# Retention's value and gate projections as seven block products

## The chip, the cores and the metric

One Trainium2 chip, one of its cores. The time is device microseconds (us) of one execution of the kernel. The engines are PE (TensorE, matmuls; PEld its weight loads), DVE (VectorE), ACT (ScalarE), POOL (GpSimd) and SP (which here only issues DMAs). Each executes its own queue in order and waits on semaphores for the others.

## The reference

One decoder layer for 512 tokens of width 1024: four retention heads beside four attention heads of 128, each query attending to its best 128 keys as an indexer chooses them, then an output projection, layer norm, a SwiGLU FFN and a second norm. Cut to what matters here:

```python
proj = x @ w_in                       # 512 x 1024 times 1024 x 4168
rq, rk, rv, rg, aq, ak, av, iq, ik, iw = jnp.split(proj, IN_SPLITS, axis=-1)
ret = retention_chunkwise(rope(rq), rope(rk), rv)      # chunks of 128 tokens
ret = (ret - mean(ret)) * rsqrt(var(ret) + 1e-5) * ret_gn_gain   # per head
ret = silu(rg) * ret
sel = top_k(sum_h(iw * relu(iq_h . ik)), 128)          # causal, per query
att = softmax_attention(rope(aq), rope(ak), av, sel)
mix = concatenate([ret, att]) @ w_out
x = layer_norm(ALPHA * x + mix)
ffn = (silu(x @ w_gate) * (x @ w_up)) @ w_down
return layer_norm(ALPHA * x + ffn)
```

Here rv (values) and rg (gate) are each x times a 1024 x 512 part of `w_in`.

## The kernel before

Nearly all matmuls work on fp32 numbers split into two fp32r parts, high and low (`split`: ACT casts the high part; the low part is the rest). `mm3` makes one product of three matmuls: high by high, high by low, low by high. In `stream` each weight array has two letters, one for each half of 1024 columns: with V the low part is a DVE subtraction (L91); with Q it is made by ACT (minus the number) and a DMA from POOL's queue that adds the number to it (L88, L89).

Stages around the change, in PE's order:

- The indexer's projection (`acc`), then `proj_feature` for c = 0 to 7: keys and queries of both groups, two halves each, 24 matmuls a half into a `pf` bank. Behind each half DVE makes three rotary products (L217 to L219) and POOL adds them (L221).
- `proj_token(1)` (retention's values rv), `proj_token(2)` (its gate; `sg` and `grg`), `proj_token(0)` (attention's values av): each takes eight weight halves, and each half feeds 24 matmuls into four `pt` banks, one for each block of 128 tokens.
- Beside them runs `side`: rotation of the indexer, its logits (PE `lg`, ACT relu, DVE sum into `score`) for query blocks 1 to 3, then `topk`: 16 steps for each block of MAX8 and MATCH_REPLACE8 on DVE, over 256, 384 and 512 keys. `retention()` is a list of steps on all engines (transposed keys `rkt`, scores `rs`, state `rkv`, output `ri`, norm, scale, gate, turn).

All of it is one thread of code that issues instructions to every engine; each engine keeps the order of issue. `run(main, pace(side, r))` steps `main` and after each of its yields takes as many steps of `side` as its costs and the rate r allow. `weight()` hands out the next half and issues the preparation of the one three ahead (`prepare`); the raw arrays rotate through three buffers, the split halves through four. DMAs from HBM are issued on SP's queue in the order of issue.

Of the kernel before, what the change touches and what calls it, by code (L numbers as in the profile page):

```python
# [53 lines left out]
def hybrid_layer_kernel(ctx: ExitStack, tc: tile.TileContext, xT, x, pos, w0, wf, wt, wo,  # L54
# [30 lines left out]
    def split(eng_lo, hi, lo, src):  # L85
        A.copy(hi, src)  # L86
        if eng_lo is None:
            A.activation(lo, src, AF.Copy, scale=-1.0)  # L88
            nc.gpsimd.dma_start(lo.bitcast(F32), src, accum_op=ALU.add)  # L89
        else:  # L90
            eng_lo.tensor_tensor(lo, src, hi.bitcast(F32), op=ALU.subtract)  # L91
# [77 lines left out]
        yield  # L169


    stream = [(wf[c], "VV" if c == 0 else "VQ") for c in range(8)]
    stream += [(wt[g, i], "QQ") for g in (1, 2, 0) for i in range(2)]
    stream += [(wo[c], "VV") for _ in range(2) for c in range(4)]
    limit = [len(stream)]
    ready, taken, raws = [], [0], []

    def fetch(n):
        while len(raws) < min(n, limit[0]):
            raws.append(wp.tile([P, 2, 1024], F32, tag="raw", name=f"raw{len(raws)}"))  # L180
            dma(raws[-1], stream[len(raws) - 1][0])

# [50 lines left out]
    def index_rope():  # L233
# [105 lines left out]

    tok = {}  # L340

    def proj_token(g):
        accs = [(psu if g == 1 and b > 1 else psd)(f"pt{g}_{b}") for b in range(NB)]

        def evac(b):
            if b == 0:
                tok[g] = unit(("s4", "s5", "s6")[g], ("av", "rv", "grg")[g])
            if g == 2:
                sg = tmp("sg")
                A.activation(sg, accs[b], AF.Silu)  # L350
                G.tensor_tensor(tok[g][:, b], sg, gnb, op=ALU.mult)
            else:
                A.copy(tok[g][:, b], accs[b])

        for c in range(4):
            h, l = weight()
            for b in range(NB):
                bs = slice(b * P, b * P + P)
                for k in range(2):
                    kt = 2 * c + k  # L360
                    ks = slice(k * S, k * S + S)
                    mm3(accs[b], xh[kt][:, bs], xl[kt][:, bs], h[:, ks], l[:, ks], kt == 0, kt == KT - 1)
                settle()
                if c == 3:
                    pending.append(lambda b=b: evac(b))
# [113 lines left out]
    def ret_state(b):  # L479
        kv = psu(f"rkv{b}")  # L480
        for h in range(HEADS):
            hs = slice(h * P, h * P + P)
            T.matmul(kv[:, hs], lhsT=rt["k", b][:, hs], rhs=tok[1][:, b, hs], start=True, stop=True)
        new = rt["state", b + 1] = tmp(f"rstate{b}")
        if b == 0:
            A.copy(new, kv)
        else:
            G.tensor_tensor(heads(new), heads(rt["state", b]), per_head(8), op=ALU.mult)
            V.tensor_tensor(new, new, kv, op=ALU.add)

    def ret_out(b, pair):
        if pair == 0:
# [9 lines left out]
    def ret_norm(b):  # L502
        st = sp.tile([P, 4, 6], F32, tag="st", name="st")
        mv = sp.tile([P, 4, 2], F32, tag="mv", name="mv")
        for h in range(HEADS):
            V.bn_stats(st[:, h], rt[b][:, h * P:(h + 1) * P])
        for h in range(HEADS):
            V.bn_aggr(mv[:, h], st[:, h])
        rt["norm", b] = mv, rstd_of(mv[:, :, 1], 4)

    def ret_scale(b):
        mv, r = rt["norm", b]
        z = tmp("rz")
        for h in range(HEADS):
            hs = slice(h * P, h * P + P)
            V.tensor_scalar(z[:, hs], rt[b][:, hs], mv[:, h, 0:1], r[:, h:h + 1], op0=ALU.subtract, op1=ALU.mult)
        rt[b] = z

    def ret_gate(b):
        zz = tmp("rzz")  # L520
        G.tensor_tensor(zz, rt[b], tok[2][:, b], op=ALU.mult)
        rt[b] = zz

    def ret_turn(b):
# [65 lines left out]
    prepare()  # L590
    prepare()
    const_loads()
    lg = chain(*[logits(j) for j in range(1, NB)])
# [5 lines left out]
    rt["decay"] = big.tile([P, 2, HEADS * P], F32, tag="s7", name="decay")  # L599
    dma(rt["decay"], decay_d)  # L600
# [1075 lines left out]
```

## Time and profile before

| what | value |
|---|---|
| time, median of 3 runs | 614.81 us (614.14 to 614.89) |
| profiled execution | 614.91 us, span 613.1 us |
| granted PE clock | 0.996 of full speed |
| features: first to last `pf` start | about 27 to 123 us |
| token projections (`pt`) | 123.8 to 207 us |
| DVE top-k steps (L402, L403) | 48 of each |
| low parts by ACT and POOL's DMA (L88, L89) | 19 |
| low parts by DVE (L91, 128x1024 weights) | 24 |

How to read it: the page gives busy time and counts of each engine, the chain of work that ended last, and groups of equal instructions with count, busy time, mean ns of one, and the idle time before them with the engine that ended it. The timeline shows the start, the duration and the instruction.

### The profile page before, as it was taken

The page shows a single profiled execution, that of the slowest core. Times are in us where ns is not written, and L with a number is a line of the kernel's source. Part 1 is how long each engine was busy: PE and PEld are TensorE (multiplying, and loading weights), DVE is VectorE, ACT ScalarE, POOL GpSimd, SP SyncE. Part 2 cuts the span into 40 slices and gives each one's busy share as a digit, 9 for nine tenths or more (in the row PEclk, how much of TensorE's full clock was granted, in tenths as well). Part 3 has the DMA queues.
Part 4 walks back from the last instruction along what each step waited for, and adds up shares of the span by engine and source line. Part 5 has one row for each costly group of instructions (what it writes and reads, how often), then busy time and mean ns, then how long its engine had stood idle before and what let it go on. Part 6 is the DMA issues. An engine that isn't in the chain of part 4 may idle for free.

```text
span 613.1 us, 9090 instructions
## 1 busy us (share of the span) xinstructions
PE 603.2 (98%) x3228; PEld 518.2 (85%) x3228; DVE 523.3 (85%) x973; ACT 350.1 (57%) x610; POOL 160.0 (26%) x171
## 2 busy tenths in 40 slices
PE   8999999999999999999999999999999999999994
PEld 7988888888888877889998888888888888888884
DVE  6897687987879877979998999999999899977856
ACT  5643444334252665777657767677677795648300
POOL 1187232421446000232123223231321021124010
PEclk9999999999999999999999999999999999999998
DMA  8878434788553773498399998988786459689502
GB/s 296 299 219 206 152 107 124 179 193 207 134 123 103 276 275 136 106 238 156 121 264 199 246 210 216 217 208 240 175 225 171 138 175 246 165 230 300 190 35 103
DMA packets 41805, 116.53 MB, mean 190 GB/s; under 512 B 4464, under 2 KB 10160, under 8 KB 36128
## 3 DMA queue, kind: packets, MB, share of 16 engines
q1 hardware_dynamic: 23056, 80.95, 38.0%
q0 software_dynamic: 17968, 33.76, 31.7%
q10 hardware_dynamic: 736, 1.25, 0.6%
q8 instruction: 25, 0.41, 0.3%
q14 instruction: 20, 0.16, 0.1%
HBM read 83.96 MB, written 2.10 MB: 140 GB/s over the span
## 4 chain that ended last, share of the span: by engine, by line
PE 89%; DVE 5%; issue 3%; ACT 1%; POOL 1%; DMA 1%; POOLq 0%; DVEq 0%
PE ga L905 11%; PE ga L908 6%; PE gc L905 5%; PE pf L95 5%; PE pf L94 5%; PE pf L96 5%; PE acc L205 4%; PE gb L905 3%; PE gc L908 3%; PE ga L915 3%; PE mx L96 2%; PE mx L94 2%; PE mx L95 2%; PE dl L94 2%; PE dl L95 2%
## 5 line engine op out<-in xcount | busy, mean ns | idle before, releaser
L86 ACT CAST wh<-raw 128x1024 fp32r<-128x1024 f32 x43 | 44.9, 1049 | 49.1 <-issue 21.6
L94 PE MATMUL pf<-xh,wh 128*128 128x512 f32 x128 | 50.0, 391 | 0.0
L95 PE MATMUL pf<-xl,wh 128*128 128x512 f32 x128 | 49.9, 390 | 0.0
L96 PE MATMUL pf<-xh,wl 128*128 128x512 f32 x128 | 49.9, 389 | 0.0
L91 DVE TENSOR_TENSOR wl<-raw,wh 128x1024 fp32r<-128x1024 f32 x24 | 29.5, 1240 | 13.8 <-ACT wh L86 13.8
L94 PE MATMUL pt<-wh,xh 128*128 128x512 f32 x96 | 39.1, 408 | 0.0
L440 POOL TENSOR_TENSOR rs<-ve,half 128x1 f32<-128x1 f32 (+1 forms) x11 | 11.8, 1069 | 103.9 <-DVE ve L439 103.7
L96 PE MATMUL pt<-wh,xl 128*128 128x512 f32 x96 | 37.5, 391 | 0.0
L95 PE MATMUL pt<-wl,xh 128*128 128x512 f32 x96 | 37.4, 390 | 0.0
L89 POOL DMA_DIRECT2D wl<-raw x19 | 16.9, 891 | 57.5 <-ACT wl L88 50.7
L96 PEld LDWEIGHTS pf<-xh,wl 128*128 128x128 f32 x128 | 24.0, 188 | 5.1
L94 PEld LDWEIGHTS pf<-xh,wh 128*128 128x128 f32 x128 | 24.0, 188 | 4.6
L95 PEld LDWEIGHTS pf<-xl,wh 128*128 128x128 f32 x128 | 24.1, 188 | 4.6
L402 DVE MAX8 m<-score 128x8 f32<-128x256 f32 (+2 forms) x48 | 26.8, 558 | 1.1
L403 DVE MATCH_REPLACE8 score<-m,score 128x256 f32<-128x256 f32 (+2 forms) x48 | 26.0, 543 | 0.0
L385 ACT ACTIVATE lg<-lg 128x256 f32<-128x256 f32 (+2 forms) x24 | 10.9, 474 | 24.6 <-PE lg L384 22.6
L830 POOL DMA_DIRECT2D firsts<-in_wgu_dram x18 | 19.2, 1084 | 20.3 <-DMA firsts<-in_wgu_dram 18.2
L89 POOL DMA_DIRECT2D slot<-hu x9 | 10.9, 1340 | 50.9 <-ACT slot L88 48.5
L96 PEld LDWEIGHTS pt<-wh,xl 128*128 128x128 f32 x96 | 18.0, 188 | 3.9
L95 PEld LDWEIGHTS pt<-wl,xh 128*128 128x128 f32 x96 | 18.1, 189 | 3.2
L94 PEld LDWEIGHTS pt<-wh,xh 128*128 128x128 f32 x96 | 18.1, 188 | 3.1
L835 POOL DMA_DIRECT2D graw<-graw x18 | 17.9, 992 | 10.4 <-DVE hu L968 3.6
(1240 smaller groups left out, 1967.4 us busy)
## 6 DMA issues: line engine op xcount, KB each, us to landing
graw<-in_wgu_dram SPq DMA_DIRECT2D x22, 1024.0 KB, 6.9
wl<-raw POOLq DMA_DIRECT2D x19, 512.0 KB, 5.9
raw<-in_wf_dram SPq DMA_DIRECT2D x8, 1024.0 KB, 6.8
raw<-in_wo_dram SPq DMA_DIRECT2D x8, 1024.0 KB, 4.9
raw<-in_wt_dram SPq DMA_DIRECT2D x6, 1024.0 KB, 5.4
r<-in_wd_dram SPq DMA_DIRECT2D x12, 512.0 KB, 5.8
firsts<-in_wgu_dram SPq DMA_DIRECT2D x18, 256.0 KB, 7.1
firsts<-in_wgu_dram POOLq DMA_DIRECT2D x18, 256.0 KB, 6.5
```

The lines of the kernel that those rows point to most:

```text
L86: A.copy(hi, src)
L89: nc.gpsimd.dma_start(lo.bitcast(F32), src, accum_op=ALU.add)
L91: eng_lo.tensor_tensor(lo, src, hi.bitcast(F32), op=ALU.subtract)
L94: T.matmul(acc, lhsT=lh, rhs=rh, start=first, stop=False, **kw)
L95: T.matmul(acc, lhsT=lh, rhs=rl, start=False, stop=False, **kw)
L96: T.matmul(acc, lhsT=ll, rhs=rh, start=False, stop=last, **kw)
L205: T.matmul(acc0[i][:, o:], lhsT=a[:, i * P:i * P + P], rhs=b[kt][:, o:], start=(kt == 0 and p == 0), stop=(kt == KT - 1 and p == 2))
L402: V.max(m8, a)
L403: V.match_replace(out=a, in_to_replace=m8, in_values=a, imm_value=TAKEN)
L830: nc.gpsimd.dma_start(firsts(n), wgu[order[n], :, 0, :S], accum_op=ALU.add)
L905: T.matmul(two(gp[n][acc]), lhsT=h[:, ws[k]], rhs=parts[q][:, :, k], start=first and k == 0, stop=False, skip_group_check=True)
L908: T.matmul(gp[n][acc][:, :Q], lhsT=l[:, ws[k]], rhs=parts[q][:, 0, k], start=False, stop=k == 3, skip_group_check=True)
```

## The change

Values and gate of the retention group become one product. X is cut into token halves and halves of the inner dimension (11, 12, 21, 22: 256 x 512), the weights into value and gate columns and the same inner halves. The eight block products become seven, with sums of blocks on both sides (Strassen's scheme in Winograd's form). Each of the seven takes two weight halves of 12 matmuls, and its result, in two banks of 128 tokens, goes with a sign into rv and grg (`after`).

- Four sums of x blocks are made by POOL (`x_sums`), from copies of x loaded again (`x_load`); each is split into two parts (`x_split`).
- The sums of weights are made in place: by DMAs of POOL's queue that add from HBM (`from_memory`), by two POOL additions (`second_sum`), and one array is loaded twice. A new letter G gives the low part of a half to POOL.
- The halves of features 2 to 7 now have Q for both letters, feature 1 VQ.
- The gate's silu and gain are no longer at the evacuation but steps of `retention()` (`gated`); the state's decay is a step of its own; the normalized retention output is scaled by ACT (16 instructions of 128x128) with a bias that DVE and POOL make.
- The first twelve steps of retention lie inside the product, the rest beside `proj_token()`, which makes attention's values alone. The top-k of query block 1 goes between the logits of blocks 2 and 3, and the rates of `pace` are others.

```diff
-    stream = [(wf[c], "VV" if c == 0 else "VQ") for c in range(8)]
-    stream += [(wt[g, i], "QQ") for g in (1, 2, 0) for i in range(2)]
+    stream = [(wf[c], ("VV", "VQ")[c > 0] if c < 2 else "QQ") for c in range(8)]
+    PAIR = len(stream)
+    stream += [(wt[1, 0], "QQ"), (wt[1, 1], "VV"), (wt[2, 0], "GV"), (wt[2, 1], "GV"), (None, "VG"), (wt[2, 0], "GV"), (None, "GV")]
+    stream += [(wt[0, 0], "VQ"), (wt[0, 1], "QQ")]
...
+    def from_memory(n, src, us=(0, 1)):
+        for u in us:
+            nc.gpsimd.dma_start(raws[PAIR + n][:, u], src[:, 2 * u:2 * u + 2].rearrange("p k c -> p (k c)"), accum_op=ALU.add)
+
+    def second_sum():
+        for u in range(2):
+            G.tensor_tensor(raws[PAIR + 2][:, u], raws[PAIR + 2][:, u], raws[PAIR + 3][:, u], op=ALU.add)
+
+    weight_sums = {1: lambda: from_memory(2, wt[1, 0]), 4: lambda: fetch(PAIR + 6), 5: second_sum,
+                   7: lambda: from_memory(5, wt[2, 1]), 8: lambda: from_memory(2, wt[1, 1], (0,)), 9: lambda: from_memory(2, wt[1, 1], (1,))}
...
-            split(V if stream[k // 2][1][k % 2] == "V" else None, h, l, raw)
+            split({"V": V, "G": G, "Q": None}[stream[k // 2][1][k % 2]], h, l, raw)
         ready.append((h, l))
+        if k - 2 * PAIR in weight_sums:
+            weight_sums[k - 2 * PAIR]()
...
+    def x_sums():
+        def tt(name, out, a, b, op):
+            G.tensor_tensor(xq[out], xq[a], xq[b], op=op)
+            xq[name] = xq[out]
+        tt("s3", "11", "11", "21", ALU.subtract)
...
+    def token_pair():
+        X = [psd(f"ptx{t}") for t in range(2)]
+        Z = [psu(f"ptz{t}") for t in range(2)]
...
+        for p, (q, first) in enumerate((("11", True), ("12", True), ("s1", True), ("s4", False), ("s2", False), ("s3", False), ("22", False))):
...
+            bank = {1: Z, 2: Y, 3: Y}.get(p, X)
+            side_of = x_side(q)
+            settle()
+            for u in range(2):
+                h, l = weight()
+                for t in range(2):
+                    for k in range(2):
+                        hi, lo = side_of(2 * u + k, t)
+                        ks = slice(k * S, k * S + S)
+                        mm3(bank[t], hi, lo, h[:, ks], l[:, ks], first and u == 0 and k == 0, u == 1 and k == 1,
+                            skip_group_check=True)
+                    settle()
+                    if u == 1:
+                        pending.append(lambda p=p, t=t: after(p, t))
+                    if (p, u, t) == (0, 0, 0):
+                        x_split("s1", "s4")
+                    elif (p, u, t) == (0, 0, 1):
+                        x_split("s4", "s6")
...
+                    yield
...
-            V.tensor_scalar(z[:, hs], rt[b][:, hs], mv[:, h, 0:1], r[:, h:h + 1], op0=ALU.subtract, op1=ALU.mult)
+            A.activation(z[:, hs], rt[b][:, hs], AF.Identity, scale=r[:, h:h + 1], bias=n[:, h:h + 1])
...
-    side = chain(index_rope(), lg, tk)
-    run(chain(*[proj_feature(c) for c in range(4)]), pace(side, 0.85))
-    run(chain(*[proj_feature(c) for c in range(4, 8)]), pace(side, 0.85))
-    run(proj_token(1), pace(side, 1.7))
...
+    lg1, lg23 = logits(1), chain(logits(2), logits(3))
+    side = chain(index_rope(), lg1, both(lg23, tk, 2), x_parts(), some(tk, 3), x_sums_in(), tk)
+    run(chain(*[proj_feature(c) for c in range(4)]), pace(side, 0.9))
+    x_load("s10", "21", "12")
+    run(chain(*[proj_feature(c) for c in range(4, 8)]), pace(side, 1.4))
...
+    run(token_pair(), pace(side, 0.8), later(pace(some(rets, 12), 0.65), 11))
     mixt[0] = unit("s8", "mrh", F32R), unit("s10", "mrl", F32R)
-    rets = retention()
-    run(proj_token(2), pace(side, 1.8), pace(rets, 1.2))
     tail = chain(rets, att_score(0))
-    run(proj_token(0), pace(tail, 1.4), pace(side, 0.55))
+    run(proj_token(), later(pace(tail, 1.6), 1), pace(side, 0.6))
```

POOL's queue around the end of the features. Before, the transfers for the low parts of weight halves (`wl<-raw`) take turns with the rotary additions of the retention queries (rqT):

```order
L89 DMA wl_1044<-raw_829 128x1024
L221 TENSOR_TENSOR rqT<-rt_1052,rt_1053 128x512
L89 DMA wl_1086<-raw_829 128x1024
L221 TENSOR_TENSOR rqT<-rt_1094,rt_1095 128x512
L89 DMA wl_1133<-raw_938 128x1024
L221 TENSOR_TENSOR rqT<-rt_1141,rt_1142 128x512
```

In the changed kernel the same stretch, from the rotary addition ahead of the second half's transfer on, reads as follows; `xqs` are the x blocks, `raw_1083` and `raw_1185` the gate's two weight arrays, and L282 adds from memory:

```order
L226 TENSOR_TENSOR rqT<-rt_1094,rt_1095 128x512
L394 TENSOR_TENSOR xqs_1074<-xqs_1074,xqs_787 128x1024
L394 TENSOR_TENSOR xqs_787<-xqs_1074,xqs_787 128x1024
L394 TENSOR_TENSOR xqs_1074<-xqs_1074 128x1024
L394 TENSOR_TENSOR xqs_787<-xqs_1074,xqs_787 128x1024
L89 DMA wl_1138<-raw_852 128x1024
L282 DMA raw_1083<-in_wt_dram 128x1024 x2
L226 TENSOR_TENSOR rqT<-rt_1148,rt_1149 128x512
```

The four sums of x and two additions from memory now stand around the second half's transfer (wl_1138). Further down, behind the last rotary addition (rt_1235), come POOL's own splits and sums:

```order
L226 TENSOR_TENSOR rqT<-rt_1235,rt_1236 128x512
L89 DMA xs_1263<-xqs_787 128x1024
L91 TENSOR_TENSOR wl_1271<-raw_1083,wh_1270 128x1024
L286 TENSOR_TENSOR raw_1083<-raw_1083,raw_1185 128x1024 x2
L91 TENSOR_TENSOR wl_1318<-raw_1185,wh_1317 128x1024
L282 DMA raw_1274<-in_wt_dram 128x1024 x2
```

These are the low parts of the fifth and the seventh half, with the second sum between them, where there were transfers before.

DVE's queue behind the rotation of the last feature half (`pf_1`). Before, only top-k steps (m and `score`) follow:

```order
L217 TENSOR_TENSOR rt_1189<-pf_1_1137,tables 128x512
L218 TENSOR_TENSOR rt_1190<-pf_1_1137,tables 64x512
L219 TENSOR_TENSOR rt_1190<-pf_1_1137,tables 64x512
L402 MAX m_1195<-score 128x8
L403 MATCH_REPLACE score<-m_1195,score 128x256
```

Now the low parts of the product's fourth (wl_1242) and sixth half (wl_1297) and of the x sum s1 (`xs_1251`) stand there, with three top-k steps between:

```order
L224 TENSOR_TENSOR rt_1236<-pf_1_1191,tables 64x512
L91 TENSOR_TENSOR wl_1242<-raw_969,wh_1241 128x1024
L91 TENSOR_TENSOR xs_1251<-xqs_787,xs_1251 128x1024
L519 MAX m_1254<-score 128x8
L520 MATCH_REPLACE score<-m_1254,score 128x384
L519 MAX m_1267<-score 128x8
L520 MATCH_REPLACE score<-m_1267,score 128x384
L519 MAX m_1290<-score 128x8
L520 MATCH_REPLACE score<-m_1290,score 128x384
L91 TENSOR_TENSOR wl_1297<-raw_1083,wh_1296 128x1024
```

DVE reaches the fourth half's split only behind the last rotation, and the sixth's behind three top-k steps. On PE's queue 24 matmul rows fewer stand in all.

More of the change, by code (lines that the diff above doesn't have):

```diff
@@ L340, in hybrid_layer_kernel, with proj_token @@
     tok = {}
-    def proj_token(g):
-        accs = [(psu if g == 1 and b > 1 else psd)(f"pt{g}_{b}") for b in range(NB)]
+    def proj_token():
+        accs = [psd(f"pt{b}") for b in range(NB)]
         def evac(b):
             if b == 0:
[L347 to L353, printed above, removed]
+                tok[0] = unit("s4", "av")
+            A.copy(tok[0][:, b], accs[b])
         for c in range(4):
@@ L366, in proj_token, with x_load @@
                 if b != 1:
+                    yield
+    xq, xs = {}, {}
+    T2 = 2 * P
+    def x_load(tag, *names):
+        t = big.tile([P, 2, 4, T2], F32, tag=tag, name=f"xq{tag}")
+        for i, q in enumerate(names):
+            tok_half, k_half = int(q[0]) - 1, int(q[1]) - 1
+            dma(t[:, i], xT[4 * k_half:4 * k_half + 4, :, T2 * tok_half:T2 * tok_half + T2].rearrange("k p c -> p k c"))
+            xq[q] = t[:, i]
+    def x_sums():
[3 more added lines that the diff above has]
+        tt("s3", "11", "11", "21", ALU.subtract)
+        yield
+        tt("s1", "21", "22", "21", ALU.subtract)
+        yield
+        tt("n2", "22", "22", "s3", ALU.add)
+        yield
+        tt("s4", "12", "n2", "12", ALU.subtract)
@@ new lines, in x_split, with x_side @@
+    def x_split(q, tag):
+        xs[q] = big.tile([P, 2, 4, T2], F32R, tag=tag, name=f"x{q}")
+        hi, lo = xs[q][:, 0], xs[q][:, 1]
+        if q == "s2":
+            A.activation(hi, xq["n2"], AF.Copy, scale=-1.0)
+            V.scalar_tensor_tensor(lo, in0=xq["n2"], scalar=-1.0, in1=hi.bitcast(F32), op0=ALU.mult, op1=ALU.subtract)
+        else:
+            split(V if q == "s1" else None, hi, lo, xq[q])
+    def x_side(q):
+        if q in ("11", "12", "22"):
+            o = T2 * (int(q[0]) - 1)
+            f = 4 * (int(q[1]) - 1)
+            return lambda k, t: [v[f + k][:, o + t * P:o + t * P + P] for v in (xh, xl)]
+        return lambda k, t: [xs[q][:, i, k, t * P:t * P + P] for i in range(2)]
@@ L508, in ret_norm @@
             V.bn_aggr(mv[:, h], st[:, h])
-        rt["norm", b] = mv, rstd_of(mv[:, :, 1], 4)
+        n = sp.tile([P, 4], F32, tag="nm", bufs=2, name="nm")
+        V.tensor_scalar(n, mv[:, :, 0], -1.0, None, op0=ALU.mult)
+        r = rstd_of(mv[:, :, 1], 4)
+        G.tensor_tensor(n, n, r, op=ALU.mult)
+        rt["norm", b] = n, r
     def ret_scale(b):
-        mv, r = rt["norm", b]
+        n, r = rt["norm", b]
         z = tmp("rz")
@@ L592, in hybrid_layer_kernel, with x_parts, some, x_sums_in @@
     const_loads()
-    lg = chain(*[logits(j) for j in range(1, NB)])
     tk = chain(*[topk(j) for j in range(1, NB)])
-    side = chain(index_rope(), lg, tk)
-    run(chain(*[proj_feature(c) for c in range(4)]), pace(side, 0.85))
-    run(chain(*[proj_feature(c) for c in range(4, 8)]), pace(side, 0.85))
-    run(proj_token(1), pace(side, 1.7))
-    rt["decay"] = big.tile([P, 2, HEADS * P], F32, tag="s7", name="decay")
-    dma(rt["decay"], decay_d)
+    def x_parts():
+        x_load("s8", "11", "22")
+        yield 0.01
+    def some(it, n):
+        for _ in range(n):
+            yield next(it)
+    def x_sums_in():
+        for _ in x_sums():
+            pass
+        yield 0.01
+    def both(main, it, every):
+        for n, c in enumerate(main):
+            yield c
+            if n % every == every - 1:
+                yield next(it)
+    lg1, lg23 = logits(1), chain(logits(2), logits(3))
[3 more added lines that the diff above has]
+    run(chain(*[proj_feature(c) for c in range(4, 8)]), pace(side, 1.4))
+    rets = retention()
+    def later(it, n):
+        for _ in range(n):
+            yield
+        yield from it
+    run(token_pair(), pace(side, 0.8), later(pace(some(rets, 12), 0.65), 11))
     mixt[0] = unit("s8", "mrh", F32R), unit("s10", "mrl", F32R)
-    rets = retention()
-    run(proj_token(2), pace(side, 1.8), pace(rets, 1.2))
     tail = chain(rets, att_score(0))
-    run(proj_token(0), pace(tail, 1.4), pace(side, 0.55))
+    run(proj_token(), later(pace(tail, 1.6), 1), pace(side, 0.6))
     drain(tail)
```

63 lines of the change are left out of this document (53 added, 10 removed).

## The prediction

> **What bounds the kernel now.** I read the page first: the busy shares, then the chain that ended last.
>
> ```profile
> PE 603.2 (98%) x3228; PEld 518.2 (85%) x3228; DVE 523.3 (85%) x973; ACT 350.1 (57%) x610; POOL 160.0 (26%) x171
> PE 89%; DVE 5%; issue 3%; ACT 1%; POOL 1%; DMA 1%; POOLq 0%; DVEq 0%
> ```
>
> The chain is PE nearly throughout. Whether PE also waits is told by the view of waits for PE, of which these three rows are all but 0.6 us:
>
> ```profile
> PE warm L188 <- DVE cold L185: 1.2, 1, 1.2
> PE as L552 <- DVE mrl L451: 0.2, 1, 0.2
> PE rz L528 <- POOL rzz L521: 0.2, 1, 0.2
> ```
>
> So the kernel is bound by PE's work, and work taken from PE counts in full, as long as PE stays fed. How near the others are to not feeding it, the table by stages shows (PE, PEld, DVE, ACT, POOL busy, granted clock, DMA share, GB/s):
>
> ```profile
> 90.00:120.00 30.00, 30.00 (x134) 24.82 (x134) 24.84 (x45) 13.24 (x18) 10.05 (x9) 1.00 0.57 141
> 120.00:150.00 30.00, 30.00 (x140) 25.00 (x139) 26.93 (x73) 12.57 (x15) 7.90 (x8) 1.00 0.82 193
> ```
>
> DVE is busy 83 to 90% here. ACT (42 to 44%) and POOL (26 to 34%) have room.
>
> **Price of the matmuls removed.** Two rows of the timeline in the first token projection, twelve matmuls apart, and their group:
>
> ```profile
> 129.71 0.39 PE L96 MATMUL pt<-wh,xl 128*128 128x512 f32 x1
> 132.43 0.39 PE L96 MATMUL pt<-wh,xl 128*128 128x512 f32 x1
> L96 PE MATMUL pt<-wh,xl 128*128 128x512 f32 x96 | 37.5, 391 | 0.0
> ```
>
> A matmul lasts 0.39 us, but the next starts 2.72 / 12 = 0.227 us after it. The value and gate projections had 192; seven products of 24 make 168. PE loses 24 x 0.227 = 5.4 us. By the mean of the group it would be 24 x 0.391 = 9.4 us, which counts overlapping time twice. The Trainium skill warns of just this ("Trainium Kernel Development and Optimization", Performance Expectations: matmul busy time is a bad metric because matmuls are pipelined); this trace agrees, 0.39 beside 0.227, and by the busy time the result would be some 4 us lower than mine. The retention matmuls only move. One step of four of them, and the split matmul behind it:
>
> ```profile
> 151.03 0.60 PE L475 MATMUL rkt<-ident,rkT 128*128 128x128 f32 x4
> 151.38 0.47 PE L94 MATMUL pt<-wh,xh 128*128 128x512 f32 x1
> 151.70 0.39 PE L95 MATMUL pt<-wl,xh 128*128 128x512 f32 x1
> ```
>
> The four take 0.35 us from start to start, and the first matmul behind them 0.32 in place of 0.23: 0.45 a step, as before, wherever the step stands.
>
> **Price of what feeds the products.** A weight half fed 24 matmuls, 5.44 us; in the pair it feeds 12, 2.72 us. I call the pair's fourteen halves h0 to h13 and set the clock to 0 where PE starts h0; half n is needed at 2.72n, its low part one matmul later (+0.23), and from h6 on the retention steps between (0.45 us each) move the need back. The rows for the feeders:
>
> ```profile
> L86 ACT CAST wh<-raw 128x1024 fp32r<-128x1024 f32 x43 | 44.9, 1049 | 49.1 <-issue 21.6 <-PE pf L95 12.2 <-PE pt L96 11.9
> L91 DVE TENSOR_TENSOR wl<-raw,wh 128x1024 fp32r<-128x1024 f32 x24 | 29.5, 1240 | 13.8 <-ACT wh L86 13.8
> L89 POOL DMA_DIRECT2D wl<-raw x19 | 16.9, 891 | 57.5 <-ACT wl L88 50.7 <-PE lg L384 6.9
> L217 DVE TENSOR_TENSOR rt<-pf,tables 128x512 f32<-128x512 f32 x16 | 10.9, 683 | 3.3 <-PE pf L96 3.3
> L470 DVE TENSOR_TENSOR rst<-rs,decay 128x512 f32<-128x512 f32 x4 | 2.7, 684 | 3.1 <-DMA decay<-in_decay_dram 3.1
> L402 DVE MAX8 m<-score 128x8 f32<-128x256 f32 x16 | 6.8, 428 | 0.5
> L402 DVE MAX8 m<-score 128x8 f32<-128x384 f32 x16 | 9.0, 559 | 0.4
> L402 DVE MAX8 m<-score 128x8 f32<-128x512 f32 x16 | 11.0, 688 | 0.1
> L403 DVE MATCH_REPLACE8 score<-m,score 128x384 f32<-128x384 f32 x16 | 8.7, 543 | 0.0
> L403 DVE MATCH_VALUE_LOAD score<-m,score 128x8 f32 x48 | 4.4, 92 | 1.7
> L506 DVE BATCH_NORM_STATS2 st<-ri 128x6 f32<-128x128 f32 x16 | 3.5, 282 | 0.0
> L516 DVE TENSOR_SCALAR rz<-ri,mv,rs 128x128 f32<-128x128 f32 x16 | 5.4, 402 | 0.0
> L353 ACT COPY rv<-pt 128x512 f32<-128x512 f32 x4 | 2.3, 577 | 1.0 <-PE pt L96 1.0
> wl<-raw POOLq DMA_DIRECT2D x19, 512.0 KB, 5.9
> L465 POOL TENSOR_TENSOR rqd<-rqT,decay 128x512 f32<-128x512 f32 x3 | 4.5, 1493 | 0.0
> L488 POOL TENSOR_TENSOR rstate<-rstate,cols 128x512 f32<-128x512 f32 x2 | 2.1, 1032 | 0.0
> raw<-in_wt_dram SPq DMA_DIRECT2D x6, 1024.0 KB, 5.4
> ```
>
> A top-k step over 384 keys is 0.56 + 0.54 + 0.09 and gaps, 1.25 us, and in the same way 0.98 over 256 and 1.5 over 512; a rotation of a feature half, three rows like L217, 2.1.
>
> *ACT*: six more casts (6.3 us), four x casts and two low parts (6.3), six more evacuations (3.5), sixteen retention scalings. These have no row on ACT; between DVE's 0.40 each and a whole 0.58 evacuation, 6 to 9. One low part fewer: about 22 us on an engine with some 17 of each 30 free. It hides; without that cover the casts would be late with the rest below.
>
> *DVE* gives up six splits of the feature weights (7.4) and the scaling (16 x 0.402 = 6.4), and gets, between the last feature and the first half of the next projection, nine 1.24 us splits (11.2), eleven top-k steps of 384 keys (13.8), two of 512 (3.0), eight 0.68 us adds and scalings (5.4), a block's statistics and small ones (3.5): 37 us of PE's 38.1 + 5 for retention. The top-k that now lies among the logits (the sixteen steps of 256 keys) loads the last four features harder.
>
> *POOL* gets eleven sums or splits of 128x1024. No such row exists; the two nearest are
>
> ```profile
> 43.74 1.29 POOL L221 TENSOR_TENSOR akT<-rt,rt 128x512 f32<-128x512 f32 x1 [0.34 <-DVE rt L219]
> 45.00 1.01 POOL L252 TENSOR_TENSOR ql<-qs,qa 128x384 fp32r<-128x384 f32 x1
> ```
>
> that is 2.1 ns an element or a little more and 1.29 + 512 x 0.0021 = 2.36 us each, 26 us in all (bounds: 2.0 by scaling only half, 2.6 as twice the short one). Six transfers that add from memory take about 1 us of its queue each.
>
> *Transfers*: 2 MB of x, 1 MB of weights read again, 3 MB added: some 6 MB over 60 us, 100 GB/s beside 141 to 193. I leave landings at 5.4 to 5.9; a few us more would be late at the same places. On SP's queue the array for h6 may load only once h1's transfer has read its buffer (3.4 below), lands at 8.8, and POOL wants it at 11.4; the decay table loads once the rotations are done (6.2), lands by 16 even if it takes 9, and the first scores are scaled after 20.
>
> *Contention.* The same mask addition on DVE, beside a running sum on POOL and alone:
>
> ```profile
> 90.99 1.59 POOL L221 TENSOR_TENSOR rkT<-rt,rt 128x512 f32<-128x512 f32 x1
> 90.96 1.78 DVE L395 TENSOR_TENSOR score<-score,masks 128x128 f32<-128x128 f32 x1
> 107.73 0.29 DVE L395 TENSOR_TENSOR score<-score,masks 128x128 f32<-128x128 f32 x1
> ```
>
> It ends with POOL's sum, 1.5 us late. DVE's splits have two SBUF operands like this one, and the new POOL sums are longer: one that meets another waits 0 to 2.4 us. The Trainium skill ("GPSIMD Engine Reference", Key points) says that GpSimd shares its SBUF interfaces with VectorE, with contention for instructions with two SBUF inputs, and would leave elementwise work to VectorE; the trace agrees with the contention, and by that advice these sums are on the wrong engine.
>
> **Where PE comes to wait.** Lateness isn't added up: the stall is the largest of (ready minus needed).
>
> 1. *h1's low part*. POOL's four x sums stand ahead of its transfer. The x halves can be asked for when the last logits are done, 15 matmuls before the feature half that starts at -16.3, at about -19.7, landing at -13; the rotation ahead of the sums on POOL ends at -12. Sums -12 to -2.5, transfer lands 5.9 later, 3.4; needed at 2.95: 0.5 late, up to 2 if DVE comes between.
>
> 2. *DVE's backlog.* In the last three feature halves of 5.44 us it has 2.1 of rotation plus four steps of 256 keys (4 x 0.98), then one, a threshold, two of 384 and a split (5.0), then three of 384 (3.75): 6.0, 7.1, 5.9, a lag of 2.7. One meeting with POOL, 1.2, on top: the last rotation ends at 6.2, not 2.3.
>
> 3. *h6's split on POOL.* After 6.2 POOL has a rotary addition (7.5), a transfer, delayed by a DVE split (9.0), h4's split (11.4; needed 11.1), a sum (13.7), then a sum that may start only when DVE has split h5. DVE: h3 (7.4; needed 8.4), an x split (8.6), three top-k steps (12.4), held by POOL's sum to 13.7, h5 ready at 14.9 (needed 13.9). POOL's second sum 17.3, h6 19.6. Needed at 16.3 + 0.23 + one retention step = 17.0: 2.6 late.
>
> 4. *h8 to h10.* DVE: two steps and two adds (18.7), h7 behind POOL (20.8), the s2 split (22.0), two steps (24.5), h8 (25.7; needed 23.8). POOL's next transfer waits for that: h9 29.0 (needed 27.0), two transfers, h10 33.2 (needed 30.0): 3.2 late. Then two retention products, 1.5 and 1.0, and h12 at 38.1 (needed 36.9): it begins to catch up.
>
> 5. *The value projection of attention* follows. Its weights take the buffer that h13's split frees, about 39; 5.4 to land, 1.05 cast, 1.24 split: 46.7, needed at 38.1 + 0.2 + twelve steps, 5.2, + 3.2 = 46.7. No further wait, with nothing to spare.
>
> Stall 3.2. With no meetings and DVE one us earlier, only h10 is late, by about 0.7; with every meeting at full length h6 and h10 go to 5 and, with the longer transfers, 7. I take 3.2, since the rows show that these meetings happen.
>
> **Sum**: the profiled execution took 614.9 (span 613.1 and 1.8 around it), 0.1 above the median. 614.8 - 5.4 + 3.2 = 612.6.
>
> **Rivals.**
>
> *Fed in time* (stall under 1): 609.4 to 610.4. For it: ACT and POOL have room on the mean. Against: items 1 and 3.
>
> *The saving is eaten*, stall 4.2 to 6.7: 613.6 to 616.0, no change. It comes about if a backlog on DVE of 2 us more meets item 3.
>
> *DVE becomes the bound*, slower. Place: h0 to h13. If each of its nine splits waits 1.5 us as at 90.96, DVE has 37 + 13.5 = 50.5 beside PE's 43, with 2.7 carried in: a stall of 10, 614.8 - 5.4 + 10 = 619.4. It decides once the mean wait passes about 1.1 us (37 + 9.9 + 2.7 - 43 = 6.6, more than the 5.4 and 1.2 together). For it: the new sums occupy POOL 26 us of some 56, so nearly every second split should meet one. Against: top-k steps, with one operand, fill most of DVE's time, and POOL also waits for transfers and casts.
>
> By the advice of the Trainium skill quoted above (sums kept off GpSimd) it would be this last case; the trace bears out the contention, not its size.
>
> **How the numbers follow.** Part of the gain kept, stall 1 to 4.2: 0.48. Fed in time: 0.12. Eaten: 0.24. DVE the bound: 0.16. Within 0.2% (1.2 us, about what a measurement here can tell from no change) lies the third: faster 0.60, same 0.24, slower 0.16. The range goes down to 609.6, where nearly all of the fed case is in, and up to 616.4, past the eaten one; about 2 in 10 stay out.
>
> **What would show it.** Right: PE's starts in the pair 0.227 apart, rows of PE waiting for wl on POOL or DVE and for the low part's transfer, 2 to 4 us in sum between the last feature and the next projection; POOL rows of 128x1024 near 2.4; DVE splits of 1.24 stretched to 2 or more; the later stages shifted only. Wrong: no such waits; or waits at the next projection's first half, or from the retention steps that now run inside the pair, above 1 us; or mean split times above 2.5 us.

## The result: 619.9 us, slower by 0.8%

The changed kernel takes 619.93 us (median of 4 runs, 619.2 to 620.51) beside 614.85 us for the kernel before: a ratio of 1.0081 (95% interval 1.0063 to 1.0099). I had forecast 612.6, in 609.6 to 616.4. The profiled execution took 619.79 us, its span 618.0.

The page after, in its busy shares and its chain that ended last:

```profile
PE 601.5 (97%) x3204; PEld 514.5 (83%) x3204; DVE 535.0 (87%) x971; ACT 369.1 (60%) x643; POOL 194.4 (31%) x193
PE 68%; DVE 11%; DMA 7%; issue 6%; POOL 4%; ACT 2%; POOLq 0%; DVEq 0%; ACTq 0%; SPq 0%
```

PE has its 24 matmuls less, but is 68% of the chain, not 89%. The view of PE's waits names the places (line, what PE waited for, us in total, times, longest):

```profile
PE pty L94 <- ACT decay L440: 2.5, 1, 2.5
PE ptx L96 <- DMA xs<-xqs: 1.4, 1, 1.4
PE pty L95 <- POOL wl L91: 1.3, 1, 1.3
...
PE ga L1064 <- DMA parts<-cs: 0.7, 1, 0.7
PE dy L95 <- DVE dlp L91: 0.6, 1, 0.6
PE pty L95 <- DVE wl L91: 0.5, 1, 0.5
```

Four rows of `pty` and `ptx` are inside the pair; two, `ga` and `dy`, lie in the FFN. Everything up to h0 starts on time (123.7 us, before 123.8). From h0 to the first matmul of attention's values there are 55.5 us. The same stretch takes 47.3 us in a run below that feeds PE well, so the pair's stall is 8.2 us. PE starts the output projection 2.95 us later than before, counted from the first feature matmul: 8.9 us worse than the 5.97 us earlier of that well fed run. The other 2 us of the loss come later: 0.5 at L1064, 0.8 at the down projection's `dy`, and small ones.

What the waits do not show is the price of a stop. After the 2.5 us the granted clock falls (columns: us, then PE, PEld, DVE, ACT, POOL busy, granted clock, DMA share, GB/s):

```profile
144.00:147.00 3.00, 1.12 (x5) 0.95 (x6) 3.00 (x2) 3.00 (x5) 2.59 (x3) 1.00 0.21 33
147.00:148.00 1.00, 1.00 (x6) 0.85 (x5) 0.97 (x4) 1.00 (x2) 0.00 (x0) 0.64 0.95 188
148.00:150.00 2.00, 2.00 (x9) 1.81 (x8) 1.93 (x5) 1.15 (x2) 0.00 (x0) 0.50 1.04 250
```

At 0.50 the matmuls of h6 start 0.42 us apart instead of 0.227. That is another 1.9 us. In this execution they are no further loss: the transfer that PE waits for at h10 landed at 164.11, and with faster matmuls PE would have waited there longer.

Beside it VectorE is full. The first row is of before, the second of after, over the same 55 us; the third and fourth are 31 us of after and of before from about the start of the output projection:

```profile
124.00:179.00 55.00, 55.00 (x294) 47.08 (x294) 47.61 (x130) 22.56 (x27) 14.04 (x15) 1.00 0.75 175
```

```profile
124.00:179.00 55.00, 49.27 (x242) 40.37 (x241) 51.98 (x87) 28.39 (x37) 35.27 (x25) 0.97 0.80 198
...
209.00:240.00 31.00, 31.00 (x152) 24.05 (x152) 30.09 (x77) 20.47 (x51) 0.00 (x0) 1.00 0.71 259
```

```profile
209.00:240.00 31.00, 31.00 (x161) 24.46 (x160) 22.19 (x50) 19.78 (x46) 0.00 (x0) 1.00 0.63 233
```

After the change DVE is busy 52 us of 55 in the pair with fewer instructions than before (87, not 130), and 30.1 of 31 while the output projection runs, not 22.2. The groups of DVE in the pair tell why fewer take longer:

```profile
L91 DVE TENSOR_TENSOR wl<-raw,wh 128x1024 fp32r<-128x1024 f32 x7 | 16.1, 2297 | 2.1 <-ACT wh L86 2.1
L519 DVE MAX8 m<-score 128x8 f32<-128x384 f32 (+1 forms) x17 | 9.8, 579 | 0.2
L450 DVE TENSOR_TENSOR decay<-decay,gx 128x512 f32<-128x512 f32 x2 | 3.2, 1584 | 0.0
```

A split has a mean of 2.30 us, not 1.24, a 0.68 us addition 1.58. And 17 rounds of the selection stand among them.

### The profile page after: what moved, and what is told of

It is laid out like the page before. It is cut to its first block, busy times and chain, and to the rows that moved or that the text cites. A ratio compares the mean times of both kernels' runs of the same rounds, so it can differ in the third digit from the quotient of the medians.

```text
span 618.0 us, 9127 instructions
## 1 busy us (share of the span) xinstructions
PE 601.5 (97%) x3204; PEld 514.5 (83%) x3204; DVE 535.0 (87%) x971; ACT 369.1 (60%) x643; POOL 194.4 (31%) x193
## 4 chain that ended last, share of the span: by engine, by line
PE 68%; DVE 11%; DMA 7%; issue 6%; POOL 4%; ACT 2%; POOLq 0%; DVEq 0%; ACTq 0%; SPq 0%
PE ga L1054 11%; PE ga L1057 6%; PE gc L1054 5%; PE pf L94 5%; PE pf L95 5%; PE pf L96 5%; PE acc L210 4%; PE gb L1054 3%; PE gc L1057 3%; DVE wl L91 3%; PE ga L1064 2%; DMA raw<-in_wt_dram 2%; PE gc L1064 2%; PE dr L96 2%; PE dr L94 2%
## 5 line engine op out<-in xcount | busy, mean ns | idle before, releaser
L86 ACT CAST wh<-raw 128x1024 fp32r<-128x1024 f32 x49 | 51.1, 1050 | 46.6 <-PE pf L95 17.8
L95 PE MATMUL pf<-xl,wh 128*128 128x512 f32 x128 | 49.9, 390 | 0.0
L91 DVE TENSOR_TENSOR wl<-raw,wh 128x1024 fp32r<-128x1024 f32 x26 | 39.3, 1523 | 10.8 <-ACT wh L86 10.8
L95 PEld LDWEIGHTS pf<-xl,wh 128*128 128x128 f32 x128 | 24.1, 188 | 4.5
L89 POOL DMA_DIRECT2D slot<-hu x9 | 10.9, 1338 | 49.1 <-ACT slot L88 49.1
L1104 DVE TENSOR_TENSOR gu<-gu,gc 128x512 f32<-128x512 f32 x18 | 12.4, 688 | 8.8 <-ACT gu L1099 8.8
L1099 ACT ACTIVATE gu<-ga 128x512 f32<-128x512 f32 x18 | 10.8, 599 | 14.0 <-PE ga L1057 14.0
L88 ACT ACTIVATE wl<-raw 128x1024 fp32r<-128x1024 f32 x18 | 19.1, 1059 | 0.0
L508 DVE SCALAR_TENSOR_TENSOR score<-lg,iw,score 128x256 f32<-128x256 f32 (+2 forms) x21 | 12.9, 615 | 7.1 <-ACT lg L502 6.3
L1099 ACT ACTIVATE gt<-ga 128x512 f32<-128x512 f32 (+1 forms) x26 | 13.8, 532 | 6.5 <-PE ga L1064 6.0
L1086 ACT ACTIVATE hu<-hu 128x256 f32<-128x256 f32 x20 | 8.0, 417 | 13.4 <-DVE hu L1076 13.4
```

The costliest lines, as they stand in the source:

```text
L95: T.matmul(acc, lhsT=lh, rhs=rl, start=False, stop=False, **kw)
```

## The experiments

Seventeen kernels, each the changed one with an edit. The pair's length is counted from PE's start of h0 to its start of attention's values (55.5 in the changed kernel). Three theories at first. A: the low halves of the x parts, which come by a transfer that takes 9.6 us, hold ACT's queue and PE. B: VectorE, with the selection, is full. C: GpSimd's sums stretch VectorE's two-operand passes.

### One suspect at a time

`e1_x_on_dve`, the low halves of all x parts on VectorE:

```diff
-            split(V if q == "s1" else None, hi, lo, xq[q])
+            split(V, hi, lo, xq[q])
```

> Theory A (the low halves of the x parts come through an accumulating DMA that lands late, and its buffer and ACT's queue hold PE): with those low halves subtracted on VectorE there is no such DMA, so the waits of PE on ACT's read-out before h6 (2.7 us, with the clock after it some 1.9 us more) and on the transfer at h10 (1.5 us) vanish; with up to 2 us back for two more subtractions of 1.2 us on VectorE the time is 614 to 616.5. Theory B (VectorE's backlog of top-k passes makes the weights' splits late): VectorE gets still more, 620 to 623. Theory C (the two-operand sums on GpSimd hold VectorE's two-operand passes): no sum is taken away, 619 to 621.

`e2_one_topk`, of each block's sixteen rounds only the first:

```diff
+            if it == 0:
                 V.max(m8, a)
                 V.match_replace(out=a, in_to_replace=m8, in_values=a, imm_value=TAKEN)
```

> Left out: fifteen of the sixteen rounds of each block's top-k selection, so that VectorE has some 90 instructions less; their places in the order stay. Theory A: the transfers land as late as before, the waits at h6 and h10 stay, and only what waits for VectorE's splits (h5, a part of h4, about 1 us) goes: 617 to 619 by the end of the token pair, less where the later selection has held something. Theory B: all of the stall but the transfers' goes, 611 to 614. Theory C: the splits still meet the sums, 617 to 620.

`e3_no_sums`, without the six additions on GpSimd:

```diff
-            G.tensor_tensor(raws[PAIR + 2][:, u], raws[PAIR + 2][:, u], raws[PAIR + 3][:, u], op=ALU.add)
-            G.tensor_tensor(xq[out], xq[a], xq[b], op=op)
```

> Left out: the four sums of x parts and the second weight sum on GpSimd (six 128x1024 additions, 2.4 us each); their inputs stand in for them. Theory A: the transfers of the x parts are issued by GpSimd's queue at much the same time and land as late, 617 to 619.5 (h4's and h5's 2.2 us may go). Theory B: 618 to 620, VectorE has as much to do. Theory C: VectorE's backlog at the start of the pair and the late splits of h4 and h5 go, 613 to 616.

`e4_no_sums_one_topk`, both:

> Left out: both of the above, fifteen of sixteen rounds of the selection and the six additions on GpSimd. Theory A: what is left of the stall is the transfers' alone, the wait before h6 and the one at h10 with the clock after them, 613.5 to 616. Theories B and C together: nothing is left of the stall, the full saving of the 24 matmuls shows, 608.5 to 611.5.

Measured: e1 621.0 us (ratio to before 1.0102, 1.0087 to 1.0118), e2 618.67 (1.0059, 1.0044 to 1.0074), e3 618.61 (1.0058, 1.0041 to 1.0075), e4 610.73 (0.9927, 0.9911 to 0.9942). Each alone is worth 1.3 us or nothing, the two together 9.2. No single theory does that. With e4 the whole saving is there: PE starts the output projection 5.97 us earlier than before, and the pair takes 47.3 us.

Theory A alone falls with e1. Its two waits are gone from the view, but others have come:

```profile
PE pty L95 <- POOL wl L91: 2.7, 2, 1.3
PE rz L653 <- POOL rzz L646: 2.0, 2, 1.8
PE pty L95 <- DVE wl L91: 1.6, 1, 1.6
PE as L677 <- DVE mrl L568: 1.3, 1, 1.3
```

The pair is 2.3 us shorter (53.3), and 3.4 us are lost again behind it, at the turns of retention (`rz`) and the first attention scores (`as`). In e2, with VectorE unburdened, the pair is no shorter (56.1 us): PE waits 3.1 us for a split of POOL and 2.1 for ACT's read-out. In e3 it is 52.8, and as in e1 most of the gain is lost behind it. Theory C falls with e3 as well: without the six sums the seven splits in the pair take 2.41 us on the mean, as changed 2.30. What stretches them there is GpSimd's other work (last section).

### GpSimd's queue and the transfers

A fourth theory, D: the transfers that add the first weight sum stand behind all four x sums in GpSimd's queue, and what follows from them is late. The timeline of POOL in the changed kernel:

```profile
116.97 2.41 POOL L394 TENSOR_TENSOR xqs<-xqs 128x1024 f32<-128x1024 f32 x1
119.45 2.40 POOL L394 TENSOR_TENSOR xqs<-xqs,xqs 128x1024 f32<-128x1024 f32 x1
121.78 0.89 POOL L89 DMA_DIRECT2D wl<-raw  x1
122.35 2.15 POOL L282 DMA_DIRECT2D raw<-in_wt_dram  x2
```

and the transfers' medians from issue to landing, where I had left 5.4 to 5.9:

```profile
raw<-in_wt_dram POOLq DMA_DIRECT2D x6, 512.0 KB, 8.4
...
xs<-xqs POOLq DMA_DIRECT2D x2, 512.0 KB, 9.6
```

`e5_mem_first` issues those two transfers ahead of the last two x sums:

```diff
-    weight_sums = {1: lambda: from_memory(2, wt[1, 0]), 4: lambda: fetch(PAIR + 6), 5: second_sum,
+    def first_sum():
+        from_memory(2, wt[1, 0])
+        for _ in xsums:
+            pass
+    weight_sums = {1: first_sum, 4: lambda: fetch(PAIR + 6), 5: second_sum,
...
-        for _ in x_sums():
-            pass
+        next(xsums)
+        next(xsums)
```

> Only the order of GpSimd's queue changes: the two transfers that add the first weight sum into raw18 (issued 1.35 and 0.80 us before PE starts h0, behind all four x sums, and landed 8.4 and 12.5 us later) are issued ahead of the last two x sums. Theory D (GpSimd's queue: what stands ahead of those transfers makes h4's and h5's splits late, and with them the second sum and all that follows): they go out some 4 us earlier, the 1.5 us before h4's low part and 0.7 us before h5's go, and part of the wait before h6: 616 to 618.5. Theory B (VectorE is full in the pair, 55.8 us busy of 55.5, whatever comes earlier waits for it): 619 to 621.

`e7_second_dma`: this, the edit of e1, and

```diff
-4: lambda: fetch(PAIR + 6), 5: second_sum,
+4: lambda: fetch(PAIR + 6), 5: lambda: from_memory(2, wt[2, 1]),
```

> Three edits: the transfers ahead of the last two x sums, as above; the low halves of all x parts on VectorE, so that no accumulating transfer holds the buffer of the second x part and with it ACT's queue; and the second weight sum as an accumulating transfer from HBM instead of two 2.4 us additions on GpSimd. Theory D: GpSimd's queue is 9.6 us lighter in the pair, most of the stall goes, 613 to 616. Theory B: VectorE has 2.4 us more and the pair stays at 54 to 56 us, 618 to 621.

`e8_pace`: as e7, and

```diff
-    run(token_pair(), pace(side, 0.8), ...)
+    run(token_pair(), pace(side, 0.4), ...)
-    run(proj_token(), later(pace(tail, 1.6), 1), pace(side, 0.6))
+    run(proj_token(), later(pace(tail, 1.6), 1), pace(side, 1.2))
```

> The three edits above, and the selection at half its pace in the pair (0.4 instead of 0.8), made up at twice the pace in the attention's value projection (1.2 instead of 0.6). Theory B: VectorE's load in the pair falls by some 10 us and the stall goes, 611 to 614, if the selection is still done in time. Theory D: the same as without it, 613 to 616, or 616 to 619 if the selection now ends late and the first attention blocks wait for it.

`f1_x_dve_one_topk`: the edits of e1 and e2 together.

> Left out: fifteen of the sixteen rounds of each block's selection; besides, the low halves of all x parts on VectorE. All sums stay on GpSimd, in their places. Theory D: h4 to h6 and h8 still wait for the weight sums, 615 to 617.5. Theory A (the x parts' transfers alone, with a full VectorE): both are gone here, 610.5 to 613.

Measured: e5 620.91 us (1.0083, 1.0066 to 1.01), e7 620.28 (1.0078, 1.0063 to 1.0093), e8 621.2 (1.0089, 1.0071 to 1.0106), f1 617.25 (1.0033, 1.0019 to 1.0048). With all rounds of the selection, easing the sums gave nothing (D misses; e5's pair takes 57.8 us, e7's 53.0, with the gain lost again behind it); with three of 48 the sums still cost (f1 is at the upper end of what D said). The waits of f1 show that second chain bare, since the x parts' transfers and VectorE's load are both out:

```profile
PE pty L95 <- POOL wl L91: 4.5, 1, 4.5
```

One stop of 4.5 us before h6's low part, and the lower clock behind it: h6 took 11.1 us instead of 3.8. In e8 the pair fell to 51.3 us, but the rounds moved behind it were waited for there (theory B misses too):

```profile
PE apt L703 <- DVE mx L684: 4.1, 2, 2.1
```

### Both eased, with every sum computed

So theory E: two chains of nearly the same length, VectorE's load on one side, the weight sums through GpSimd's queue and its transfers on the other. `g1_second_dma_one_topk` is e7 with one of sixteen rounds:

> Left out: fifteen of the sixteen rounds of each block's selection. Besides, the three edits to the weight and x sums (first sum's transfers ahead of the last two x sums, all x low halves on VectorE, second weight sum by a transfer). All sums are computed, so this is the whole pair with VectorE relieved. Theory E (two chains of nearly the same length: VectorE's load, and the weight sums through GpSimd's queue and its transfers; relieving one leaves the other): both are eased here, the pair takes 47.5 to 50 us and the time is 609.5 to 612.5. Theory D alone (the sums' queue, not eased by these edits): 614 to 617.

It took 611.4 us (0.9939, 0.9923 to 0.9956), the pair 48.7. Four cells and their neighbours:

| selection | sums on GpSimd as changed | sums eased |
|---|---|---|
| 48 rounds | 619.9 | 620.3 (e7), 618.6 (left out, e3) |
| 3 rounds | 618.7 (e2), 617.3 (f1) | 611.4 (g1), 610.7 (left out, e4) |

Each side hides the other. The idle time of DVE ahead of its splits in the pair (last columns, with what ended it) agrees; the rows are those of e7, g1 and f1 in this order:

```profile
L91 DVE TENSOR_TENSOR wl<-raw,wh 128x1024 fp32r<-128x1024 f32 x8 | 16.0, 1995 | 0.0
```

```profile
L91 DVE TENSOR_TENSOR wl<-raw,wh 128x1024 fp32r<-128x1024 f32 x7 | 15.2, 2174 | 3.6 <-ACT wh L86 3.6
```

```profile
L91 DVE TENSOR_TENSOR wl<-raw,wh 128x1024 fp32r<-128x1024 f32 x7 | 12.7, 1819 | 7.8 <-ACT wh L86 7.8
```

With all rounds (e7) DVE never waits for a cast, PE waits for DVE. With three, DVE waits. The splits stay stretched (2.17 us in g1) and do no harm when DVE has time. From f1 to g1 only GpSimd's queue differs (the order of the transfers, and the second sum as a transfer): 5.9 us.

### How much VectorE lacks, and whether order gives it back

`i1_twelve_rounds`: e7 with twelve of each sixteen rounds (`if it % 4 != 3`).

> Left out: four of the sixteen rounds of each block's selection, some 13 us of VectorE's passes; besides, the three edits to the sums. With all 48 rounds this kernel took 620.3, with three 611.4. Theory F (VectorE lacks a fixed amount, about 9 us, and what it is spared beyond that is idle): the deficit is about covered, 611.5 to 614. Rival (each round counts where it stands, in proportion): a quarter of the 8.9 us, 617.5 to 618.5.

613.19 us (0.9959, 0.9936 to 0.9983; the runs spread from 609.6 to 615.0). By the medians a quarter of the rounds gives 7.1 of the 8.9 us that nearly all give: no proportion, but what a fixed lack of some 7 to 9 us would give. That is the forecast of the theory now called F (VectorE's total load up to the end of attention); that it is this total which counts is not shown by it.

If it is the total, order cannot mend it. `g2_wo_vq` and `g3_wo_qq` slow the selection in the pair as in e8 and take splits of the output weights from VectorE (both on top of e7; rates 0.5 and 1.0, then 0.4 and 1.2):

```diff
-    stream += [(wo[c], "VV") for _ in range(2) for c in range(4)]
+    stream += [(wo[c], "VQ" if i == 0 else "VV") for i in range(2) for c in range(4)]
```

with "QQ" in place of "VQ" in g3.

> Nothing left out. The three edits to the sums, the selection at 0.5 of a step in the pair and 1.0 in the attention's value projection, and four of the first eight splits of the output weights through ScalarE and a transfer instead of VectorE: VectorE has 4.9 us less before the last attention block. Theory E (VectorE is full from the pair to the end of attention, so that what it is spared comes off the end): 621.2 of the slowed selection falls by about 4 to 6, 615 to 617.5. Rival (the wait of the attention is on ScalarE or the transfers): 619 to 622.

> Nothing left out. As the last, with the selection at 0.4 and 1.2 and all eight of the first splits of the output weights through ScalarE and a transfer: VectorE has 9.8 us less. Theory E: 611.5 to 614.5, faster than before the change, the first version in which its saving shows. Rival (ScalarE, at 20 us busy of 31 while the mixture is projected, gets 8.5 us more and becomes what the attention waits for): 617 to 621.

620.54 us (1.0094, 1.0079 to 1.0109) and 620.51 (1.0089, 1.0067 to 1.011): both miss E's figures and lie where the rival put them. The pair is at 51.6 to 51.7 us, but attention waits behind it: from the first matmul of the output projection to the first of the FFN it is 69.8 us in g2 and 69.7 in g3, beside 71.9 in e8 and 65.4 as changed, though VectorE has 9.8 us less to do there in g3. (e8's profiled execution took 623.05 us, more than its median, g3's 618.61, less.) Of PE's waits in g3:

```profile
PE apt L703 <- ACT apts L705: 1.1, 1, 1.1
...
PE rz L658 <- POOL rzz L651: 0.8, 1, 0.8
PE apt L703 <- DVE mx L684: 0.8, 1, 0.8
...
PE mx L95 <- DMA wl<-raw: 0.5, 1, 0.5
```

The wait for DVE in attention went from 4.1 to 0.8, but ACT, POOL and a transfer are waited for in its place: what was taken from VectorE came to ACT and the transfers, which are needed there as well. So VectorE's total alone, as theory F has it, does not tell the time either.

The other way round, the selection earlier. `h7_early_selection` changes rates alone (0.9, 1.4, 0.8 and 0.6 become 1.4, 1.6, 0.5 and 0.5), `h4_early_and_sums` adds the edits of e1 and the second sum by a transfer, `h5_earlier_and_sums` takes 1.4, 1.8, 0.4 and 0.5.

> Only the places of the index logits, the selection and the x sums in the order change: the side work runs at 1.4 and 1.6 in the feature projections (0.9 and 1.4 as changed) and at 0.5 in the pair and after it (0.8 and 0.6), so that 30 of the 48 rounds, not 18, stand ahead of the pair's first split on VectorE; the x sums come earlier with them. Theory E (two chains: VectorE's rounds inside the pair, and GpSimd's sums ahead of the transfers): both are partly eased, 613 to 617. Theory F (VectorE's total load up to the end of attention): the rounds ahead of the pair push the features' rotations, 619 to 622.

> The same places, and besides the low halves of all x parts on VectorE and the second weight sum by an accumulating transfer. Theory E: the pair comes to 48.5 to 51 us and little is waited for behind it, 610.5 to 614, faster than before the change. Theory F: 618 to 622.

> As the last, with the side work at 1.8 in the second half of the feature projections and 0.4 in the pair: 33 of 48 rounds stand ahead of the pair. Theory E: within 1 us of the last, 610 to 614, if VectorE still has room ahead of the pair; Theory F: 619 to 623, PE then waits for the rotations in the feature projections.

628.08 us (1.0237, 1.0181 to 1.0294), 620.99 (1.01, 1.0085 to 1.0115) and 628.97 (1.0224, 1.0164 to 1.0284). The 10.9 idle us of VectorE between 50 and 80 us were used (26.3 busy of 30 in h7, 19.1 as changed), and the stall came earlier and larger. In h7:

```profile
PE ptz L95 <- DVE wl L91: 6.4, 1, 6.4
```

```profile
80.00:100.00 20.00, 20.00 (x90) 16.57 (x89) 18.37 (x44) 10.43 (x13) 8.42 (x7) 1.00 0.92 228
100.00:124.00 24.00, 24.00 (x108) 19.87 (x107) 23.05 (x51) 7.08 (x7) 16.61 (x13) 1.00 0.74 178
124.00:140.00 16.00, 9.58 (x43) 7.64 (x42) 15.49 (x30) 7.91 (x9) 4.18 (x4) 0.94 0.55 132
```

DVE (the third busy time) is full from 100 us on, the last rotation ends 13.7 us after h0 starts, and h3's split comes behind it. In h4 the x sums, in one piece and earlier than as changed, stand ahead of the features' weight transfers; they cost PE 2.6 us of waits in the features and the clock behind them, which is why it is no faster although its pair is at 51.6. `h8_spread_sums` (rates as h4) and `h9_spread_sums_slower` (1.2, 1.5, 0.6, 0.55) put rounds of the selection between the x sums:

```diff
         for _ in x_sums():
-            pass
+            yield next(tk)
+            yield next(tk)
```

> Nothing left out. The selection earlier (1.4 and 1.6 in the feature projections, 0.5 in the pair and after), x low halves on VectorE, second weight sum by a transfer, and the four x sums not in one piece but two by two with weight splits' transfers between them, so that the 2.6 us of PE's waits on those transfers in the feature projections go, with some 2 us of the clock behind them. Theory F: what VectorE lacks shows elsewhere, 617 to 620. Theory E: 613.5 to 616.

> As the last, but 1.2 and 1.5 in the feature projections, 0.6 in the pair and 0.55 after it: 26 rounds ahead of the pair instead of 30. Theory F: 617 to 620, the order matters little. Theory E: 614 to 617.

624.71 us (1.0191, 1.0139 to 1.0244) and 623.28 (1.013, 1.0109 to 1.0151), outside both ranges. The waits for the transfers shrink to 0.5 us in h8, and h3's split is 5.9 and 5.6 us late instead. No version that keeps all rounds beat the kernel before, and every order tried moved the stall only. This fits F, but it does not show that no order can do it, and F's figures were too low four times (h5, h7, h8, h9). One reason is the clock, which they left out: in h7 the stop of 6.4 us ahead of h3's low part cost 2.4 us more, until h4, by slower matmuls.

## Why the prediction was wrong

*Price of the matmuls*: right. Fed well, PE reaches the output projection 4.6 (g1) to 6.0 us (e4) earlier than before; 5.4 was forecast.

*POOL's 128x1024 sum*: 2.36 forecast, 2.40 measured. *ACT*: a retention scaling takes 0.46 us, inside the bounds of 0.40 and 0.58. *Item 1*, h1's low part: 0.5 late forecast, 0.24 measured. *Item 2*: the last rotation ended at 7.1, not 6.2.

*Items 3 and 4* are the step that failed: they follow the low parts of the weights alone, and leave out two other things that a half needs. (Lateness here is against e4's clock, in which PE hardly waits.) The first is the bank. h6 was 4.9 us late, not 2.6, since PE waited for ACT's read-out of the bank `pty`. It stood in ACT's queue behind the cast of the x part s2, and that behind a transfer that still read its buffer. ACT's timeline:

```profile
143.34 1.06 ACT L409 ACTIVATE xs<-xqs 128x1024 fp32r<-128x1024 f32 x1 [4.96 <-DMA xs<-xqs]
144.30 1.03 ACT L86 CAST wh<-raw 128x1024 fp32r<-128x1024 f32 x1
145.23 1.08 ACT L440 ACTIVATE decay<-pty 128x512 f32<-128x512 f32 x2
```

The second is the other operand. h10's weights were ready at 35.0 (33.2 forecast), 2.9 late, beside 3.2 forecast; but PE waited for the low part of the x part s3. POOL's queue ahead of its transfer:

```profile
150.92 0.87 POOL L282 DMA_DIRECT2D raw<-in_wt_dram  x1 [4.33 <-DVE wl L91]
151.49 2.74 POOL L91 TENSOR_TENSOR wl<-raw,wh 128x1024 fp32r<-128x1024 f32 x1
154.52 0.88 POOL L282 DMA_DIRECT2D raw<-in_wt_dram  x1 [0.30 <-PE pty L95]
155.09 1.22 POOL L89 DMA_DIRECT2D xs<-xqs  x1
```

POOL waited for DVE's split of h8, then made its own of h9; the transfer was issued at 155.09 and landed 9.0 us later, 40.4 on the prediction's clock. It was needed at 32.4. In item 4 this landing costs nothing: "two transfers" there are their time in POOL's queue. The term behind both is *landings of 5.4 to 5.9 us*, of which I had said that "a few us more would be late at the same places": the x parts' two transfers took 10.1 and 9.0, and were late at places that I had not listed. The 5.9 is a median; in the kernel before single landings of that row ran from 4.5 to 10.7 us.

*"Lateness isn't added up: the stall is the largest of (ready minus needed)"* held here. The stops were 1.5 us at h4's low part, 0.7 at h5's, 2.7 at h6 and 1.5 at h10, with 1.9 by the clock between the last two; but each is only what the next input was later still. The last one, 8.0 late, gives the stall of 8.2, and POOL's queue ahead of it waited for PE for 0.30 us at most. What the rule leaves out is the clock behind the last stop. In f1, where nothing later is waited for, h6's low part is 4.7 late and the pair loses 7.4.

The needs were mis-sized too, in the safe direction: the twelve retention steps in the pair take about 8.9 us (47.3 of e4, less 38.1 for the products and 0.3 of waiting), not 5.2, as those of eight matmuls cost about 0.9.

*DVE's load in the pair*: 37 us forecast, 52.5 of 55.5 measured (its rows, some of which overlap, add up to 56; the 55.8 of an expectation above is such a sum). Seventeen rounds, not thirteen, add 5; its nine 128x1024 passes took 19.6 us instead of 11.2, a mean wait of 0.93; an addition of 0.68 us took 2.49. This load is the second term that failed: e1 takes the x parts' transfers away, and the pair still takes 53.3 us, 6.0 more than in e4. The rival "DVE becomes the bound" gave 619.4, from a wait of 1.5 a pass and a chance of 0.16. That it comes so near is in part luck: the mean wait was shorter than its turning point of 1.1, and with VectorE relieved alone (e2) the time is still 618.7. It had neither the additional rounds nor the second chain. With GpSimd's sums eased (e7) DVE is what is left: i1 and g1, which differ from e7 by rounds alone, are 7.1 and 8.9 us faster.

*Item 5*, no wait at attention's value projection: right as far as PE's waits go. What lies behind it I had not costed: DVE's 30.1 of 31 us until attention ends, where e1, e3 and e7 gave back what they had gained in the pair, and about 1 us in the FFN.

## What to carry to other kernels

Work taken from the bound engine is a gain only if the feeders' whole load, summed to the point where its last result is needed, fits into the shorter time; a stage's mean with its stretched passes tells more than a count of instructions. Where two feeding chains are about equally late, undoing either one shows nothing: leave out both, then each, before you call a suspect innocent. And before the largest lateness is taken, list for each piece of work all that it needs: both operands and the bank that must have been read, not only the part that has changed.

## What the runs showed of the hardware

A DVE split that takes 1.22 us alone can take many times that beside GpSimd. Here it began at 157.86, met four POOL instructions, each begun before the one ahead had ended, and ended at 164.39, 1.1 us after the last of them (POOL's rows in a fence of their own):

```profile
157.86 6.53 DVE L91 TENSOR_TENSOR wl<-raw,wh 128x1024 fp32r<-128x1024 f32 x1 [2.06 <-ACT wh L86]
```

```profile
155.66 3.07 POOL L91 TENSOR_TENSOR wl<-raw,wh 128x1024 fp32r<-128x1024 f32 x1
158.03 1.95 POOL L582 TENSOR_TENSOR rqd<-rqT,decay 128x512 f32<-128x512 f32 x1
159.25 1.71 POOL L610 TENSOR_TENSOR rstate<-rstate,cols 128x512 f32<-128x512 f32 x1
160.40 2.90 POOL L91 TENSOR_TENSOR wl<-raw,wh 128x1024 fp32r<-128x1024 f32 x1
```

The splits at 137.82 and 143.58 (2.27 and 2.40 us) also ended 1.1 us after the POOL instruction that ran when they began. In g1 POOL's instructions from 126.73 to 132.50 left no pause either, and yet two DVE passes got in between them, in 2.30 and 2.31 us; what decides that is open. None of the four instructions above is one of the six sums, and no run took GpSimd's own splits away. The selection's rounds, with one operand, kept their 0.55 to 0.69 us throughout. The clock's fall to 0.50 for some 3 us after a stop of 2.5 us I had not priced. The Trainium skill ("TensorE: Matmul & The Clock Gate", HAM oscillation) puts the harm at gaps of more than about 3.4 us; here one of 2.5 us, after two shorter ones, was enough. Open is why the changed kernel and most of its versions lose about 0.7 us at `dy` (L95, waiting for DVE's `dlp`), far behind the edits; e3, e4, e5, e7, g3 and h9 do not, and no run was made for it.
